# Split passes for the first S5 layer's products, with two u tiles and one tile of reordered states

## The chip, the cores and the metric

The kernel runs on one core of a Trainium2 chip. The metric is the device time of one execution, in microseconds (us). The core has TensorE (PE in the rows; PEld is its weight load), VectorE (DVE), ScalarE (ACT), GpSimd (POOL) and SyncE (SP), which mostly issues DMAs. Each engine runs its own instructions in the order in which they stand, and waits at one whose operands are not ready.

## The reference

The program is one inference step of a network of four layers over 128 context and 256 latent tokens, 384 together, of 1024 channels. Each layer norms its input, modulates it with a shift and a scale from a conditioning vector, mixes, gates and projects back. Layer 0 and layer 3 mix with an S5 state-space model, layer 1 pools, layer 2 attends. The S5 layer in its core:

```
u, z = split(h @ w_in, 2)                  # h: 384 x 1024, u and z: 384 x 2048
lam_bar = exp(lam * step)                  # for each of 128 groups, 64 states, 2 directions
b_bar = ((lam_bar - 1) / lam) * b
bu = einsum('blgc,gpc->blgp', u, b_bar)
states = associative_scan(a_r * a_l, a_r * b_l + b_r)   # forward and backward in time
y = d_skip * u + sum over directions of real(einsum(states, c))
y = gelu(y); y = y * sigmoid(y @ glu_w + glu_b)
out = (y * silu(z)) @ w_out
```

All arrays are float32.

## The kernel before

The first S5 layer is `S5Body.run`. Its 128 groups go in four blocks of 32. For block b, `u` (line 1074) multiplies h by four units of 128x1024 weights into three PSUM banks and VectorE transposes these into a tile of `Us`, one of three that blocks use in turn. `win` (four per block, q = 0 to 3) masks a quarter of the u tile on ScalarE (L1113), multiplies it by the input matrices on TensorE (L1122) and copies the result into E on ScalarE (L1125). E holds a block's states; two E buffers are used in turn, so block 2 needs the one of block 0. `rec` runs the scan in place in E: 63 steps of three VectorE operations (Pr, R, E; line 51 is the helper that issues them), where the first 32 steps work on two segments and the last 31, the half steps, on one.

When a block's scan is done, `out` makes four tiles of outputs (q = 0 to 3): `in_time` copies the states into an Eq tile in another order, with one copy of 64 partitions for each direction (L1185, L1188; on ScalarE, in block 3 the first of the two on VectorE), then TensorE multiplies in four groups Eq by P (L1212) and u by M (L1208), ScalarE applies the gelu (L1215) and issues the DMA of the result to yd. P and M are made on VectorE and TensorE by `S5Prep` from the layer's parameters. Eq has two buffers; in block 3 two tiles of `Us` stand in for two of its four Eq tiles.

z has sixteen units, each a product of 128x1024 weights with h on TensorE (L204), a silu on ScalarE (L1095) and a DMA; 3, 4, 3 and 6 of them are listed at the ends of the four scans.

The kernel has two ways to multiply in nearly float32. In `prod_a32` and `prod_b32` TensorE takes the float32 operands as they are, and each matmul leaves two records in the trace. In `prod_a` and `prod_b` each operand is the sum of a rounded high part and a low part, and three passes (high by high, high by low, low by high) are added in PSUM: `unit` casts the weights on ScalarE (whi, L138) and subtracts on VectorE (wlo, line 51). Before, the first S5 layer uses the former and all other layers the latter. The second S5 layer (`ahead`) has its own body, whose tables and some of whose low parts are made earlier and read back.

The ring of 128x1024 tiles has three slots each for whi and wlo. The tables of `S5Prep` in the first layer (W, and w1, w2, t) take slots of the same two names.

The order of the work on each engine is set by a list scheduler when the program is built: `run` gives it the steps of a block with the step of the scan at which each is listed, and it may move an instruction ahead of others on its engine where data allow.

Of the kernel before, what the change touches and what calls it, by code (L numbers as in the profile page):

```python
# [9 lines left out]
F32 = mybir.dt.float32  # L10
F32R = mybir.dt.float32r
# [19 lines left out]
class Net:  # L31
# [160 lines left out]
            if done:  # L192
                done(T, pss[T])

    def raw_unit(self, src):
        raw = self.ring.tile([128, 1024], F32, name="raw", tag="raw", bufs=4)
        self.nc.sync.dma_start(raw, src)
        return raw

    def prod_a32(self, ps, src, x):  # L200

        w = self.raw_unit(src)
        for k in range(8):
            self.nc.tensor.matmul(ps, w[:, k * 128:(k + 1) * 128], x[:, k, :], start=k == 0, stop=k == 7)  # L204

    def prod_b32(self, pss, wsrc, x):

        for u in range(4):
            w = self.raw_unit(wsrc[u])
            for k in range(2):  # L210
                kk = 2 * u + k
                for T, ps in enumerate(pss):
                    self.nc.tensor.matmul(ps, x[:, kk, T * 128:(T + 1) * 128], w[:, k * 512:(k + 1) * 512],  # L213
                                          start=kk == 0, stop=kk == 7)


    def rstd(self, xs, n, sqs):

# [41 lines left out]
    def modulated(self, l, hT, xn, natural=False):  # L260
# [3 lines left out]
        for k in range(8):  # L264
            ps = self.bank(self.sp, "sp")
            for T in range(3):
                nc.tensor.transpose(ps[:, T * 128:(T + 1) * 128], xn[:, T, k * 128:(k + 1) * 128], self.ident)
            p3 = ps[:, :NT].rearrange("p (t c) -> p t c", t=3)

            def put(out, act):  # L270
                o = out.rearrange("p (t c) -> p t c", t=3)
                if natural:

                    hv = o.rearrange("p t (c s) -> p t s c", s=4)
                    pv = p3.rearrange("p t (s c) -> p t s c", s=4)
                    dst, src = (hv[:, 0:2], hv[:, 2]), (pv[:, ::2], pv[:, 1])
                else:
                    dst, src = (o[:, ::2, :], o[:, 1, :]), (p3[:, ::2, :], p3[:, 1, :])
                for i in range(2):
                    sc, sh = m["sc"][:, k, i:i + 1], m["sh"][:, k, i:i + 1]  # L280
                    if act:
                        nc.scalar.activation(out=dst[i], in_=src[i], func=AF.Identity, scale=sc, bias=sh)
                    else:
                        nc.vector.tensor_scalar(out=dst[i], in0=src[i], scalar1=sc, scalar2=sh, op0=OP.mult, op1=OP.add)

            if hl is None:
                put(hh[:, k, :], k % 2)
                continue
            h = self.work.tile([128, 512], F32, name="h", tag="yo")[:, :NT]
            put(h, k % 2)  # L290
            if k % 2:
                nc.scalar.copy(out=hh[:, k, :], in_=h)
            else:
                put(hh[:, k, :], True)
            self.tt(hl[:, k, :], h, hh[:, k, :].bitcast(F32), OP.subtract)
# [161 lines left out]
    def s5(self, l, j, before, fill, ahead, side, between):  # L457
# [3 lines left out]
        with ExitStack() as outer:  # L461
# [7 lines left out]
            eps = [outer.enter_context(tc.tile_pool(name=f"ep{i}", bufs=1)) for i in range(2 if ahead else 1)]  # L469
            glu = Glu(self, j, yd, zd, eps)  # L470
            with ExitStack() as body:
                self.xn = eps[0].tile([128, 3, D], F32, name="xn", tag="e")
                h = []

                def start():
                    before()
                    xn = self.normed()
                    h.append(self.xp.tile([128, 8, NT], F32, name="h", tag="x"))
                    self.modulated(l, (h[0], None), xn)

                b = (S5Skewed if ahead else S5Body)(self, j, yd, zd, eps, body, ahead, start)
                if ahead:
                    before()
                    xn = self.normed()
                    h = [self.xp.tile([128, 8, NT], F32R, name="hh", tag="x"), b.sb.tile([128, 8, NT], F32R, name="hl")]
                    self.modulated(l, h, xn)
                b.run(h if ahead else h[0], fill, glu)
            self.x = self.xp.tile([128, 3, D], F32, name="x", tag="x")
            between()
            pp = outer.enter_context(tc.tile_pool(name="pp", bufs=1, side="right"))  # L490
# [541 lines left out]
class S5Body:  # L1032
# [3 lines left out]
    def __init__(self, net, j, yd, zd, eps, ctx, ahead, start):  # L1036
# [28 lines left out]
            self.prep.pair = lambda: (wq.tile([128, 4, 2, 64], F32, name="M", tag="M"),  # L1065
                                      wq.tile([128, 4, 64], F32, name="Md", tag="Md", bufs=1))
        self.eps = eps
        self.Us = [sb.tile([128, 16, 96], F32, name=f"U{i}") for i in range(3)]
        self.h0 = net.load(sb, A["h0"][j], [128, 64, 2, 2], "h0")
        nc.scalar.mul(out=self.h0[:, :, :, 1], in_=self.h0[:, :, :, 1], mul=-1.0)  # L1070
        self.fin = sb.tile([128, 64, 2, 2], F32, name="fin")
# [1 line left out]
    def u(self, b):  # L1073
# [1 line left out]
        n = self.n  # L1075
        pss = [n.bank(n.acc, "acc") for _ in range(3)]
        w = self.A["s5_wu"][self.j, b]
        if self.ahead:
            n.prod_b(pss, w, 4, *self.h, los=[self.ahead.lod[4 * b + u] if 4 * b + u < self.ahead.ulo else None for u in range(4)])
        else:  # L1080
            n.prod_b32(pss, w, self.h)
        U = self.Us[b % len(self.Us)]
        for T in range(3):
            self.nc.vector.transpose(out=U[:, :, T * 32:T * 32 + 32], in_=pss[T].rearrange("p (q c) -> p q c", c=32))
# [1 line left out]
    def z(self, q):  # L1086
        n, nc = self.n, self.nc
        ps = n.bank(n.acc, "acc")[:, :NT]
        w = self.A["s5_wz"][self.j, q]
        if self.ahead:  # L1090
            n.prod_a(ps, [w], 1, *self.h, los=[self.ahead.lod[16 + q] if q < self.ahead.zlo else None])
        else:
            n.prod_a32(ps, w, self.h)
        sz = n.work.tile([128, NT], F32, name="sz", tag="sz")
        nc.scalar.activation(out=sz.rearrange("p (s k c) -> p k s c", k=3, s=4),  # L1095
                             in_=ps.rearrange("p (k s c) -> p k s c", k=3, s=4), func=AF.Silu)
# [91 lines left out]
        nc.scalar.copy(out=ev[64:128, :, 3 - k - m:3 - k], in_=raw_ap(E[64:128], o, [[1, 16], [-33 * 64, m], [-64, 32]]))  # L1188

    def eq(self, b, qq):  # L1190
        if b == 3 and qq in (1, 2):
            return self.Us[qq]
        return self.wq.tile([128, 16, 96], F32, name="Eq", tag="Eq", bufs=1 if self.ahead else 2)

    def chunk_out(self, b, qq, P, M, Eq=None):

# [337 lines left out]
```

## Time and profile before

| what | value |
|---|---|
| median of three runs | 1810.89 us (1810.05 to 1817.27) |
| profiled execution | 1812.23 us, span 1810.4 us |
| mean granted clock of TensorE | 0.963 of full speed |
| busy: TensorE, VectorE, ScalarE | 1686.1, 1254.9, 978.3 us |

A row of a timeline gives the start from the span's beginning, the length, the engine, the line in the kernel, the operation, the tile written and those read with shapes, the number of instructions merged into it, and in brackets how long the engine idled before it and which engine's instruction ended that. The clock of TensorE is told as a share of 2.4 GHz. Ends of matmuls are modelled, so a last one shows its latency too. The first S5 layer's body runs from 47.6 to about 480 us: the first block's u and inputs to 80.8, scans of blocks 0 and 1 to 208.1, outputs of block 0 to 240.4, then inputs of block 2, and so on.

### The profile page before, as it was taken

Reading aid. Unit: us, or ns where it says so; the run is one execution under the profiler, and the core shown is the slowest. Engines: PE = TensorE matmul, PEld = TensorE weight load, DVE = VectorE, ACT = ScalarE, POOL = GpSimd, SP = SyncE. Lnnn points to the kernel's source line nnn. Section 1 sums busy time; section 2 is a strip of 40 time slices with the busy share of each in tenths; the row PEclk is TensorE's granted clock in tenths of the full one; section 3 lists DMA queues with packets and bytes.
Section 4 is the critical chain, followed back from the end, with each engine's and each line's share of the span. In section 5 each row is a group of like instructions: output and inputs, shape, how many; then the busy total and the mean of one; then the engine's idle time right before and its main releaser. Section 6 shows DMA issues by size and latency. Waiting matters only on the chain.

```text
span 1810.4 us, 29493 instructions
## 1 busy us (share of the span) xinstructions
PE 1686.1 (93%) x10928; PEld 1318.4 (73%) x10928; DVE 1254.9 (69%) x3149; ACT 978.3 (54%) x1588; POOL 5.4 (0%) x16
## 2 busy tenths in 40 slices
PE   4999999998999998999998999999899999899998
PEld 1464454654799977999887885657678778689986
DVE  7699876787476567888867737763439978656435
ACT  2653487636654455655546555642354777754322
POOL 0000000000000000000000000000000000000000
PEclk7999999997899998999998999999999999799999
DMA  8337767654577664655563566732567754567552
GB/s 311 98 119 240 228 182 220 195 180 137 166 252 231 193 205 135 188 162 163 179 218 113 186 205 229 239 127 82 181 226 226 227 182 140 166 232 213 172 165 72
DMA packets 174831, 334.30 MB, mean 185 GB/s; under 512 B 78528, under 2 KB 101856, under 8 KB 174688
## 3 DMA queue, kind: packets, MB, share of 16 engines
q1 hardware_dynamic: 165728, 319.84, 55.6%
q10 hardware_dynamic: 8960, 12.59, 2.1%
q8 instruction: 86, 1.41, 0.3%
q14 instruction: 57, 0.47, 0.1%
HBM read 279.54 MB, written 52.82 MB: 184 GB/s over the span
## 4 chain that ended last, share of the span: by engine, by line
PE 72%; DVE 9%; ACT 9%; DMA 6%; issue 3%; SPq 0%; ACTq 0%; DVEq 0%
PE acc L175 6%; PE acc L177 6%; PE acc L176 6%; PE sp L1122 4%; PE acc L829 4%; PE acc L830 4%; PE acc L831 4%; PE acc L213 3%; PE acc L159 3%; PE acc L160 3%; PE acc L161 3%; PE acc L204 3%; ACT Eq L1188 3%; DMA adw<-in_ada_w 2%; PE adps L99 2%
## 5 line engine op out<-in xcount | busy, mean ns | idle before, releaser
L51 DVE TENSOR_TENSOR wlo<-raw,whi 128x1024 fp32r<-128x1024 f32 (+2 forms) x234 | 281.2, 1204 | 246.3 <-ACT whi L138 229.0
L138 ACT CAST whi<-raw 128x1024 fp32r<-128x1024 f32 x246 | 257.6, 1050 | 315.2 <-PE acc L177 130.0
L51 DVE TENSOR_TENSOR Pr<-E,Tb 128x256 f32<-128x256 f32 (+1 forms) x504 | 173.9, 354 | 9.3 <-ACT E L1131 3.3
L159 PE MATMUL acc<-hh,whi 128*128 128x384 f32 x512 | 177.3, 347 | 0.2
L161 PE MATMUL acc<-hh,wlo 128*128 128x384 f32 x512 | 174.3, 340 | 0.3 <-DVE wlo L51 0.2
L160 PE MATMUL acc<-hl,whi 128*128 128x384 f32 x512 | 174.3, 340 | 0.0
L829 PE MATMUL acc<-y,whi 128*128 128x384 f32 x448 | 152.7, 345 | 8.1 <-ACT y L146 5.8
L831 PE MATMUL acc<-y,wlo 128*128 128x384 f32 x448 | 152.0, 340 | 1.0 <-DVE wlo L51 1.0
L830 PE MATMUL acc<-y,whi 128*128 128x384 f32 x448 | 152.7, 342 | 0.1
L175 PE MATMUL acc<-whi,ph 128*128 128x512 f32 x384 | 152.5, 397 | 0.0
L176 PE MATMUL acc<-wlo,ph 128*128 128x512 f32 x384 | 151.4, 394 | 0.0
L177 PE MATMUL acc<-whi,pl 128*128 128x512 f32 x384 | 151.3, 394 | 0.0
L51 DVE TENSOR_TENSOR E<-R,E 128x128 f32<-128x128 f32 (+1 forms) x504 | 123.1, 254 | 31.5 <-ACT E L1125 25.2
L51 DVE TENSOR_TENSOR R<-Pr 128x128 f32<-128x128 f32 (+1 forms) x504 | 123.7, 255 | 5.8
L159 PEld LDWEIGHTS acc<-hh,whi 128*128 128x128 f32 x512 | 97.1, 190 | 5.2 <-issue 2.0
L204 PE MATMUL acc<-h,raw 128*128 128x384 f32 x256 | 98.8, 516 | 0.0
L161 PEld LDWEIGHTS acc<-hh,wlo 128*128 128x128 f32 x512 | 96.8, 189 | 2.1 <-DVE wlo L51 0.9
L160 PEld LDWEIGHTS acc<-hl,whi 128*128 128x128 f32 x512 | 97.1, 190 | 1.0 <-issue 0.3
L99 PE MATMUL adps<-adw,scond 128*32 128x256 f32 x768 | 70.6, 422 | 27.7 <-DMA adw<-in_ada_w 27.3
L213 PE MATMUL acc<-raw,h 128*128 128x512 f32 x192 | 95.8, 617 | 0.0
L829 PEld LDWEIGHTS acc<-y,whi 128*128 128x128 f32 x448 | 84.6, 190 | 11.6 <-ACT y L146 7.1
L831 PEld LDWEIGHTS acc<-y,wlo 128*128 128x128 f32 x448 | 84.9, 190 | 2.2 <-DVE wlo L51 1.6
(285 smaller groups left out, 3261.6 us busy)
## 6 DMA issues: line engine op xcount, KB each, us to landing
adw<-in_ada_w SPq DMA_DIRECT2D x96, 512.0 KB
raw<-in_s_glu SPq DMA_DIRECT2D x64, 512.0 KB
raw<-in_s_wu SPq DMA_DIRECT2D x48, 512.0 KB
raw<-in_s_wz SPq DMA_DIRECT2D x40, 512.0 KB
raw<-in_s_wo SPq DMA_DIRECT2D x32, 512.0 KB
yq<-yd SPq DMA_DIRECT2D x64, 192.0 KB
lod<-wlo SPq DMA_DIRECT2D x24, 512.0 KB
wlo<-lod SPq DMA_DIRECT2D x24, 512.0 KB
```

The costliest lines, as they stand in the source:

```text
L51: return self.nc.vector.tensor_tensor(out=out, in0=a, in1=b, op=op)
L138: nc.scalar.copy(out=hi, in_=raw)
L159: nc.tensor.matmul(ps, h, xh[:, kk, :ncol], start=i == 0, stop=False)
L160: nc.tensor.matmul(ps, h, xl[:, kk, :ncol], start=False, stop=False)
L161: nc.tensor.matmul(ps, l, xh[:, kk, :ncol], start=False, stop=i == n - 1)
L175: nc.tensor.matmul(ps, xh[:, kk, xs], h, start=kk == 0, stop=False)
L176: nc.tensor.matmul(ps, xh[:, kk, xs], l, start=False, stop=False)
L177: nc.tensor.matmul(ps, xl[:, kk, xs], h, start=False, stop=kk == 2 * nu - 1)
L204: self.nc.tensor.matmul(ps, w[:, k * 128:(k + 1) * 128], x[:, k, :], start=k == 0, stop=k == 7)
L829: self.nc.tensor.matmul(ps, h, y[:, 0, k], start=u == 0 and k == 0, stop=False)
L830: self.nc.tensor.matmul(ps, h, y[:, 1, k], start=False, stop=False)
L831: self.nc.tensor.matmul(ps, l, y[:, 0, k], start=False, stop=u == 1 and k == 7)
```

## The change

The first S5 layer takes the same way as the others: `u` calls `prod_b` and `z` calls `prod_a`, with no low parts prepared (`los` is a list of None). `modulated` therefore makes h in two parts, hh and hl; the plain branch and the two float32 products are removed, and `start` is the same for both layers. hl takes a tile of 12 KB in each partition. `Us` has two tiles in place of three in the first layer, so that block 2 takes the tile of block 0 and block 3 that of block 1, and Eq one buffer in place of two. In block 3 only q = 1 has a u tile as its Eq.

```diff
@@ class Net
-    def raw_unit(self, src):
-        raw = self.ring.tile([128, 1024], F32, name="raw", tag="raw", bufs=4)
...
-    def prod_a32(self, ps, src, x):
...
-    def prod_b32(self, pss, wsrc, x):
...
@@ def modulated
-            if hl is None:
-                put(hh[:, k, :], k % 2)
-                continue
             h = self.work.tile([128, 512], F32, name="h", tag="yo")[:, :NT]
@@ the S5 layer
+                hlp = body.enter_context(tc.tile_pool(name="hlp", bufs=1))
...
-                    h.append(self.xp.tile([128, 8, NT], F32, name="h", tag="x"))
-                    self.modulated(l, (h[0], None), xn)
+                    h.extend([self.xp.tile([128, 8, NT], F32R, name="hh", tag="x"), hlp.tile([128, 8, NT], F32R, name="hl")])
+                    self.modulated(l, h, xn)
...
@@ class S5Body
-        self.Us = [sb.tile([128, 16, 96], F32, name=f"U{i}") for i in range(3)]
+        self.Us = [sb.tile([128, 16, 96], F32, name=f"U{i}") for i in range(3 if ahead else 2)]
...
-        if self.ahead:
-            n.prod_b(pss, w, 4, *self.h, los=[self.ahead.lod[4 * b + u] if 4 * b + u < self.ahead.ulo else None for u in range(4)])
-        else:
-            n.prod_b32(pss, w, self.h)
+        lo = lambda i: self.ahead.lod[i] if self.ahead and i < self.ahead.ulo else None
+        n.prod_b(pss, w, 4, *self.h, los=[lo(4 * b + u) for u in range(4)])
...
-        if self.ahead:
-            n.prod_a(ps, [w], 1, *self.h, los=[self.ahead.lod[16 + q] if q < self.ahead.zlo else None])
-        else:
-            n.prod_a32(ps, w, self.h)
+        n.prod_a(ps, [w], 1, *self.h, los=[self.ahead.lod[16 + q] if self.ahead and q < self.ahead.zlo else None])
...
-        if b == 3 and qq in (1, 2):
-            return self.Us[qq]
-        return self.wq.tile([128, 16, 96], F32, name="Eq", tag="Eq", bufs=1 if self.ahead else 2)
+        if b == 3 and qq in ((1, 2) if self.ahead else (1,)):
+            return self.Us[qq if self.ahead else 0]
+        return self.wq.tile([128, 16, 96], F32, name="Eq", tag="Eq", bufs=1)
```

The removed lines shift those behind them: L1185, L1188, L1208, L1212 and L1084 of before are L1154, L1157, L1177, L1181 and L1056 after. The scheduler then gives another order on each engine. Three places follow, with the rows before first and those after second; the number behind a name counts tiles, so one tile has different numbers in the two.

On ScalarE, at the end of the first block's scan (E_615 before, E_646 after), where the outputs of block 0 begin; M is the matrix for u, yc the gelu's result:

```order
L1153 ACTIVATE fin_614<-E_616 128x32 x2
L1185 COPY Eq_1963<-E_615 64x1536
L1188 COPY Eq_1963<-E_615 64x1536
L1185 COPY Eq_1999<-E_615 64x1536
L1188 COPY Eq_1999<-E_615 64x1536
L957 ACTIVATE M_1991<-Md_1992,masks_91 128x4x64
L1215 ACT_TABLE_LOAD
L1215 ACTIVATE yc_1987<-tp_1966 128x384
L957 ACTIVATE M_1991<-Md_1992,masks_91 128x4x64
L1219 DMA yd0_120<-yc_1987 4x16x384 x2
L1215 ACTIVATE yc_2023<-ad_2002 128x384
L1185 COPY Eq_2035<-E_615 64x1536
```

```order
L1154 COPY Eq_2182<-E_646 64x1536
L1157 COPY Eq_2182<-E_646 64x1536
L1122 ACTIVATE fin_645<-E_647 128x32 x2
L931 ACTIVATE M_2210<-Md_2211,masks_91 128x4x64
L1184 ACT_TABLE_LOAD
L1184 ACTIVATE yc_2206<-tp_2185 128x384
L931 ACTIVATE M_2210<-Md_2211,masks_91 128x4x64
L1188 DMA yd0_120<-yc_2206 4x16x384 x2
L1154 COPY Eq_2218<-E_646 64x1536
L1157 COPY Eq_2218<-E_646 64x1536
```

Before, four copies into two Eq tiles stand in a row, and the third tile's stand behind two gelus. After, two copies stand ahead of the first gelu, and each next tile's two copies stand behind the one before it.

On TensorE, ahead of the first products of block 1's outputs (Eq_3077 before, Eq_3440 after); adps is the product of the next layer's conditioning, sp that of `win`:

```order
L1122 MATMUL sp_2934<-U1_2912,W_2897 64x96 x4
L1122 MATMUL sp_2944<-U0_2910,W_2897 64x96 x4
L1122 MATMUL sp_2944<-U1_2912,W_2897 64x96
L99 MATMUL adps_2719<-adw_2740,scond_85 32x256 x4
L1122 MATMUL sp_2944<-U1_2912,W_2897 64x96 x3
L1212 MATMUL tp_3080<-Eq_3077,P_2163 64x96 x4
L1208 MATMUL tp_3080<-U1_609,M_2188 128x96
L1212 MATMUL tp_3080<-Eq_3077,P_2163 64x96 x4
```

```order
L160 MATMUL acc_3399<-hl_433,whi_3402 128x384
L161 MATMUL acc_3399<-hh_432,wlo_3403 128x384
L159 MATMUL acc_3399<-hh_432,whi_3402 128x384
L160 MATMUL acc_3399<-hl_433,whi_3402 128x384
L161 MATMUL acc_3399<-hh_432,wlo_3403 128x384
L1181 MATMUL tp_3443<-Eq_3440,P_2446 64x96 x4
L1177 MATMUL tp_3443<-U1_641,M_2471 128x96
L1181 MATMUL tp_3443<-Eq_3440,P_2446 64x96 x4
L1177 MATMUL tp_3443<-U1_641,M_2471 128x96
```

Before, the inputs of block 2 (win, L1122) stand right ahead of these products. After, it is the last of four z products (acc_3399), three of whose like stand above it.

On VectorE, near the end of block 3's scan (E_616 before, E_647 after), the last P, the output matrix:

```order
L51 TENSOR_TENSOR Pr_4920<-E_616,Tb_132 128x128
L51 TENSOR_TENSOR R_4921<-Pr_4920 128x2x32
L51 TENSOR_TENSOR E_616<-R_4921,E_616 128x64
L1185 COPY Eq_4927<-E_616 64x1536
L1185 COPY U1_609<-E_616 64x1536
L51 TENSOR_TENSOR adarow_4587<-adps_4586,adarow_4587 128x256
L51 TENSOR_TENSOR P_4659<-C_4657,Lf_133 128x512 x2
L51 TENSOR_TENSOR t_4660<-C_4657,Lf_133 128x512 x2
L51 TENSOR_TENSOR P_4659<-P_4659,t_4660 128x512 x2
```

```order
L51 TENSOR_TENSOR E_647<-R_5030,E_647 128x64
L51 TENSOR_TENSOR Pr_5034<-E_647,Tb_135 128x128
L51 TENSOR_TENSOR P_5146<-C_5144,Lf_136 128x512
L51 TENSOR_TENSOR R_5035<-Pr_5034 128x2x32
L51 TENSOR_TENSOR P_5146<-C_5144,Lf_136 128x512
L51 TENSOR_TENSOR E_647<-R_5035,E_647 128x64
L51 TENSOR_TENSOR P_5146<-P_5146,t_5147 128x512
L51 TENSOR_TENSOR Pr_5039<-E_647,Tb_135 128x128
L51 TENSOR_TENSOR P_5146<-P_5146,t_5147 128x512
L51 TENSOR_TENSOR R_5040<-Pr_5039 128x2x32
```

Before, the last step of the scan, the two copies and a sum stand ahead of the last P. After, that P (P_5146) stands between steps of the scan, 24 half steps ahead of its end.

## Rows read from the trace of the kernel before

**Rows 1.** The page: busy time, share of the span and instructions; then the chain's shares.

```profile
PE 1686.1 (93%) x10928; PEld 1318.4 (73%) x10928; DVE 1254.9 (69%) x3149; ACT 978.3 (54%) x1588; POOL 5.4 (0%) x16
...
PE 72%; DVE 9%; ACT 9%; DMA 6%; issue 3%; SPq 0%; ACTq 0%; DVEq 0%
```

**Rows 2.** First layer by stretch: stretch, length, busy of each engine, PE clock, DMA.

```profile
47.60:80.80 33.20, 30.67 (x95) 13.91 (x96) 19.28 (x43) 22.24 (x71) 1.68 (x2) 0.93 0.21 63
80.80:208.10 127.30, 122.71 (x1029) 65.97 (x1029) 114.07 (x382) 51.48 (x110) 0.15 (x1) 1.00 0.62 196
208.10:240.40 32.30, 28.94 (x228) 17.36 (x226) 21.59 (x57) 29.63 (x19) 0.15 (x1) 1.00 0.58 174
240.40:304.20 63.80, 60.28 (x621) 34.05 (x621) 45.23 (x128) 56.05 (x78) 0.00 (x0) 1.00 0.66 198
304.20:392.50 88.30, 86.31 (x732) 48.42 (x731) 76.39 (x277) 34.56 (x72) 0.15 (x1) 1.00 0.70 223
392.50:452.40 59.90, 47.96 (x309) 28.44 (x308) 41.55 (x143) 43.05 (x45) 0.00 (x0) 0.74 0.38 114
sum 404.80, PE 376.88 PEld 208.16 DVE 318.11 ACT 237.02 POOL 2.14; mean PE 62.81 PEld 34.69 DVE 53.02 ACT 39.50 POOL 0.36
```

**Rows 3.** Timeline, TensorE, the products now: start, length, engine, line, operation, records, [idle].

```profile
104.08 14.86 PE L213 MATMUL acc<-raw,h 128*128 128x512 f32 x34
...
206.40 2.85 PE L204 MATMUL acc<-h,raw 128*128 128x384 f32 x8
```

**Rows 4.** Timeline, TensorE, split passes of later layers.

```profile
718.92 0.33 PE L159 MATMUL acc<-hh,whi 128*128 128x384 f32 x1
...
720.48 0.34 PE L159 MATMUL acc<-hh,whi 128*128 128x384 f32 x1
...
1320.76 0.40 PE L175 MATMUL acc<-whi,hh 128*128 128x512 f32 x1
...
1322.15 0.39 PE L175 MATMUL acc<-whi,hh 128*128 128x512 f32 x1
```

**Rows 5.** Groups by shape, first 500 us: count | busy us, mean ns | idle.

```profile
L51 DVE TENSOR_TENSOR wlo<-raw,whi 128x1024 fp32r<-128x1024 f32 x7 | 8.4, 1222 | 15.5 <-ACT whi L138 9.0 <-DMA szq<-zd 6.5
L138 ACT CAST whi<-raw 128x1024 fp32r<-128x1024 f32 x8 | 8.3, 1043 | 7.3 <-DMA szq<-zd 3.7 <-PE acc L830 2.8 <-PE sp L830 0.8
```

**Rows 6.** Timeline, ScalarE, first block's outputs.

```profile
208.14 2.90 ACT L1185 COPY Eq<-E 64x1536 f32<-64x1536 f32 x1 [2.96 <-DVE E L51]
211.05 2.92 ACT L1188 COPY Eq<-E 64x1536 f32<-64x1536 f32 x1
213.99 2.90 ACT L1185 COPY Eq<-E 64x1536 f32<-64x1536 f32 x1
...
220.34 1.28 ACT L1215 ACT_TABLE_LOAD   x1
...
240.44 0.24 ACT L1131 COPY E<-h 128x64 f32<-128x64 f32 x1
```

**Rows 7.** Timeline, TensorE, one output tile at either clock.

```profile
230.07 0.55 PE L1212 MATMUL tp<-Eq,P 128*64 128x96 f32 x8 [1.48 <-ACT Eq L1188]
...
232.69 0.55 PE L1212 MATMUL tp<-Eq,P 128*64 128x96 f32 x8
...
415.78 0.91 PE L1212 MATMUL tp<-Eq,P 128*64 128x96 f32 x8 [4.52 <-ACT Eq L1188]
...
420.32 0.91 PE L1212 MATMUL tp<-Eq,P 128*64 128x96 f32 x8
```

**Rows 8.** Timeline, VectorE, third and fourth blocks.

```profile
283.84 0.29 DVE L51 TENSOR_TENSOR E<-R,E 128x128 f32<-128x128 f32 x1 [7.24 <-ACT E L1125]
...
316.21 0.72 DVE L1084 STREAM_TRANSPOSE U<-acc 128x512 f32<-128x512 f32 x1 [0.41 <-PE acc L213]
...
447.90 0.29 DVE L51 TENSOR_TENSOR Pr<-E,Tb 128x128 f32<-128x128 f32 x1
...
452.72 0.23 DVE L51 TENSOR_TENSOR E<-R,E 128x64 f32<-128x64 f32 x1
```

More of the change, by code (lines that the diff above doesn't have):

```diff
@@ L193, in prod_b @@
                 done(T, pss[T])
-    def raw_unit(self, src):
-        raw = self.ring.tile([128, 1024], F32, name="raw", tag="raw", bufs=4)
-        self.nc.sync.dma_start(raw, src)
-        return raw
-    def prod_a32(self, ps, src, x):
-        w = self.raw_unit(src)
-        for k in range(8):
-            self.nc.tensor.matmul(ps, w[:, k * 128:(k + 1) * 128], x[:, k, :], start=k == 0, stop=k == 7)
-    def prod_b32(self, pss, wsrc, x):
[L208 to L214, printed above, removed]
     def rstd(self, xs, n, sqs):
@@ L477, in start @@
                     xn = self.normed()
-                    h.append(self.xp.tile([128, 8, NT], F32, name="h", tag="x"))
-                    self.modulated(l, (h[0], None), xn)
+                    h.extend([self.xp.tile([128, 8, NT], F32R, name="hh", tag="x"), hlp.tile([128, 8, NT], F32R, name="hl")])
+                    self.modulated(l, h, xn)
                 b = (S5Skewed if ahead else S5Body)(self, j, yd, zd, eps, body, ahead, start)
                 if ahead:
[L483 to L487, printed above, removed]
+                    start()
+                b.run(h, fill, glu)
             self.x = self.xp.tile([128, 3, D], F32, name="x", tag="x")
```

## The prediction

> **What bounds the kernel now.** I read the page's first part and its chain first. TensorE is busy 93% of the span and holds 72% of the chain, VectorE 69% and 9% [rows 1]. That average covers four layers, and the change touches only the first, which lies between 47.6 and about 480 us. So the second view is the table by stretch [rows 2]. In the stretches where scans run (80.8 to 208.1 and 304.2 to 392.5 us) TensorE is busy 122.7 of 127.3 and 86.3 of 88.3 us, but VectorE is nearly as full: 114.1 of 127.3 and 76.4 of 88.3. Over the six stretches VectorE is idle 404.8 - 318.1 = 86.7 us. A busy TensorE here is partly work put into gaps: the scan is a chain of steps of three VectorE operations that nothing shortens. At its end, six half steps run from 447.90 to 452.95, 0.84 us each, with nothing between them [rows 8].
>
> The third view is the timeline of each engine where a block of the scan hands over. After the first block's last step, ScalarE reorders the states in a row of copies: 208.14, 211.05, 213.99, each 2.9 us, started by VectorE's E [rows 6]. The next scan in the same E buffer gets its first column at 240.44 [rows 6] and its last block of inputs at 283.84, after 7.24 us in which VectorE waited for ScalarE's copy [rows 8]. So the layer is set by a relay: scan (VectorE), copies (ScalarE), small products (TensorE), inputs of the scan after next (all three), scan again.
>
> **The change part by part.**
>
> *The products on TensorE.* u: 96 float32 matmuls, 192 records. 34 records take 14.86 us, the last one ending late by its own length, so (14.86 - 0.62)/33 = 0.43 us a record and 83 us in all; z: 8 records in 2.85, so 0.33, and 256 x 0.33 = 85 us [rows 3]. Split in three, u has 288 passes at (1322.15 - 1320.76)/6 = 0.232, 67 us, and z 384 at (720.48 - 718.92)/9 = 0.173, 67 us [rows 4]. TensorE has 34 us less to do. I count them as no gain in themselves, because the relay and not the queue of products sets the end; they can be worth between 0 and -34.
>
> *The splits.* Each of the 32 units of weights now needs one cast on ScalarE (1.04 us) and one subtraction on VectorE (1.22 us) before its matmuls [rows 5]: 33 us of ScalarE and 39 us of VectorE. The modulated input gets its own low part: 8 subtractions of 128x384, which the trace shows here in no such form; a third of the length of the 128x1024 one is 0.4 us, a half 0.6, so 3 to 5 us of VectorE, and about 4 of ScalarE. VectorE carries some 42 us more. The bounds of what of that lengthens the layer are 0 (all inside the 86.7 us idle) and 42.
>
> *One tile of reordered states for two.* In the first order piece ScalarE now fills one Eq, and can't fill the next before TensorE has read the first. Each tile costs 5.8 us of copies [rows 6] and then 4 groups of products, from 230.07 to about 233.5, 3.5 us at full clock; where the clock was half, from 415.78 to about 422, 6 us [rows 7]. Before, the copies of the next tile hid the groups.
>
> *Two u tiles for three.* Block 2's u now lands in block 0's tile, so its three transposes (0.72 us each [rows 8]) wait until the last product of out(0) has read it; block 3's wait for out(1). In out(3) one u tile in place of two takes reordered states. The low parts and the scan's own tables share a ring of three slots, so a table can wait for a product's last pass; I allow 0 to 7 us for that and take none.
>
> A rule speaks the other way. TensorE's weight loads are busy 73%, VectorE 69% [rows 1]. The Trainium skill, Perfetto Trace Analysis, Identifying the Most-Contended Engine, says to find the engine with the highest occupancy, TensorE judged by its weight loads, and to relieve that first. On the whole page this picks TensorE, and the sum would be -34. By stretch, weight loads are 208 of 405 us and VectorE 318 [rows 2]; the same rule read there picks VectorE, which the change loads. I go by the stretches.
>
> The relay after the change, on the profiled run's clock:
>
> 1. Scan 0 ends at 208.1 now. Ahead of it stand 11 of the 32 subtractions, 13 us, and about 5 us of the new input work: 226. Stretch 2 has 13 us of idle VectorE, so this could be as little as +5.
> 2. out(0): four times 5.8 us of copies, between them three times 3.5 us of groups and about 1 us of signals and M, and the table load 1.3 [rows 6]: 38 us, to 264. The last group (3.5) and the three transposes (2.1) bring block 2's input work to 270. It started at 240.4.
> 3. The inputs of block 2 took 240.4 to 283.8, 43 us, with 11 of copies and activations of out(0) and z mixed in; these are gone from there, so 32: 302. Already +18.
> 4. out(1) stands on TensorE behind four z products now (second order piece; TensorE runs in order): 96 x 0.173 = 17 us, which begin when their subtractions are made. First group done at 323, three more tiles at 5.8 + 3.5 + 1 and a table, 355, transposes 357. They stood at 316.2 + 0.7 [rows 8]: +40. Queued behind these transposes on VectorE is scan 2 itself, with 34 of its 63 steps to go.
> 5. Inputs of block 3, 36 us: 393. The rest of scan 2 runs beside them and ends by about 416, where it ended at 392.5: +23.
> 6. out(2): 38 + 3.5 = 457 at full clock, 467 at half; I take 460.
> 7. In the third order piece the output matrix of out(2)'s last products' slot, P, is rewritten in the middle of scan 3, and 24 half steps stand behind it on VectorE. P waits for that product; then 24 x 0.84 = 20, six subtractions 7 and a few sums of the next product's input, 4: 491. Scan 3 ended at 452.95: +38.
> 8. out(3) has one tile less to copy into: between 0 and +4. ScalarE is by then also behind later work, and I leave the total at +38.
>
> As a cross-check, VectorE's own sum is +42 with its idle time unchanged; the two counts share no term but the subtractions. Everything after the layer is the same work, so it moves as a whole. The profiled execution took 1812.23 us for a span of 1810.4, and the median of the runs is 1810.89, 1.3 less. So 1812.2 + 38 - 1.3 = 1849; I give 1848.
>
> **Rivals.**
>
> *TensorE is the bound after all.* For it: 93% busy and 72% of the chain [rows 1], 86.3 of 88.3 in stretch 5. Mechanism: products fill TensorE up to each hand-over, splits go into the 86.7 us of VectorE's idle time, and the relay moves up with them. It decides if the subtractions fit into VectorE's waits, that is, if z's go out before the scan ends rather than at it. Price: -34, so 1777, and 1780 to 1790 if out's copies give back part. Against it: stretch 6, where TensorE is 12 us idle, and the order pieces.
>
> *The splits hide, the products aren't the bound.* VectorE idle 86.7 against 42; the single Eq tile's groups (four blocks of three groups, 3.5 each, 42 us) would be paid for by the 34 us saved. Sum about +2 to +8: 1812 to 1819. Against it: the idle of VectorE is scattered, and its longest part comes after the scans, where the relay already waits.
>
> *The clock falls.* In stretch 6 the granted clock was 0.74, with TensorE busy 48 of 60 us; in the four others before it 1.00 [rows 2]. With 34 us less work in a layer 38 us longer, TensorE has more pauses in every stretch. At 1.2 instead of 2.4 GHz the z products ahead of out(1) cost 17 more and each of four outputs 2.5 more on its exposed last group, 10 in all: +27 on top, 1875. For it: the row of 415.78. Against it: TensorE keeps over 85% of its work.
>
> *The change doesn't do what it says.* The scheduler still puts three blocks' u into the air: excluded by the code, two tiles are two tiles.
>
> **How the numbers follow.** Likeliest, chance 0.62: the relay with splits in it, 1848, its own range 1828 to 1866 (step 1 at +5 gives 13 less, table waits 7 and half clock in out(2) 10 more). Clock falls as well: 0.20, 1860 to 1880. Splits hide: 0.10, 1810 to 1822. TensorE the bound: 0.08, 1777 to 1800. A measurement of this kernel can't tell less than 0.5%, 9 us, from no change: faster is under 1802, slower over 1820. Faster 0.08, same 0.09, slower 0.83. The range leaves out the TensorE case, half of the hidden case and the top of the clock case: 1815 to 1876.
>
> **What would show it.** In the changed profile the subtractions number 32 more at about 1.2 us, and TensorE is busy some 34 us less. The first copy of out(0) starts near 226. Copies of Eq stand apart in pairs with TensorE's L1181 as the releaser of the second pair. The transposes L1056 of block 3 come near 357. Scan 3 ends near 491, and from there to the end both traces run in parallel. The prediction is wrong if scan 0 ends before 212, if the layer's scans end less than 15 us later, or if the difference arises after the layer, in code that the change doesn't touch.

## The result: 74 us slower, and the profile after

The changed kernel takes 1884.87 us (median of four, 1884.52 to 1886.11) against 1810.47 for the kernel before: 1.0414 times as long, interval 1.0396 to 1.0433. The forecast was 1848, +38, with a range of 1815 to 1876. The sign was right; the size was half, and the time lies above the range.

The first part of the page of the changed kernel, busy time and then the chain's shares:

```profile
PE 1682.5 (89%) x11152; PEld 1376.9 (73%) x11152; DVE 1300.2 (69%) x3189; ACT 1014.7 (54%) x1632; POOL 5.4 (0%) x16
...
PE 66%; ACT 11%; DVE 11%; DMA 8%; issue 3%; ACTq 0%; SPq 0%; DVEq 0%
```

Against [rows 1] VectorE has 45.3 us more work (1300.2 - 1254.9), and its idle time, span less busy, rose from 555.5 to 583.1, by 27.6. TensorE's busy time hardly moved (1682.5 for 1686.1), although by the prediction's estimate it has 34 us less to do at full clock: from 47.6 us to scan 3's end its mean granted clock fell from 0.96 to 0.83, and that took the saving back. The table by stretch says where, cut at the same events as [rows 2]: prelude, first two scans, outputs of block 0, inputs of block 2, scan 2 with out(1), then out(2) and scan 3.

```profile
47.60:80.80 33.20, 28.94 (x121) 19.20 (x121) 21.64 (x48) 25.57 (x75) 1.69 (x2) 0.87 0.23 78
80.80:231.10 150.30, 117.90 (x1123) 81.88 (x1122) 128.63 (x387) 64.69 (x131) 0.15 (x1) 0.92 0.60 183
231.10:277.10 46.00, 21.82 (x152) 15.62 (x152) 31.44 (x88) 33.29 (x28) 0.15 (x1) 0.54 0.15 40
277.10:316.70 39.60, 36.33 (x450) 25.55 (x450) 21.84 (x64) 31.84 (x59) 0.00 (x0) 0.86 0.49 147
316.70:448.40 131.70, 113.09 (x999) 79.80 (x998) 105.61 (x320) 70.17 (x102) 0.15 (x1) 0.91 0.63 202
448.40:531.10 82.70, 60.49 (x425) 46.38 (x426) 61.71 (x180) 50.90 (x58) 0.00 (x0) 0.69 0.42 121
sum 483.50, PE 378.58 PEld 268.42 DVE 370.88 ACT 276.46 POOL 2.14; mean PE 63.10 PEld 44.74 DVE 61.81 ACT 46.08 POOL 0.36
```

The first scans take 150.3 us for 127.3, with VectorE 14.6 us busier and TensorE idle for 32 us where it was idle for 4.6. During the outputs of block 0 TensorE works 21.8 of 46.0 us at a granted clock of 0.54, where it had 1.00 [rows 2]. VectorE's idle time in the layer up to scan 3's end goes from 86.8 to 112.6 us.

ScalarE's timeline at the first output tiles of block 0:

```profile
231.08 2.84 ACT L1154 COPY Eq<-E 64x1536 f32<-64x1536 f32 x1 [36.48 <-DVE E L51]
233.92 2.82 ACT L1157 COPY Eq<-E 64x1536 f32<-64x1536 f32 x1
...
243.26 0.49 ACT L1184 ACTIVATE yc<-tp 128x384 f32<-128x384 f32 x1
...
245.50 2.82 ACT L1154 COPY Eq<-E 64x1536 f32<-64x1536 f32 x1 [1.35 <-issue]
```

It answers to [rows 6]: the second tile's copies begin 14.4 us after the first's, not 5.8. TensorE's timeline of the same tiles:

```profile
236.80 0.91 PE L1181 MATMUL tp<-Eq,P 128*64 128x96 f32 x8 [17.55 <-ACT Eq L1157]
...
241.33 0.91 PE L1181 MATMUL tp<-Eq,P 128*64 128x96 f32 x8
...
251.20 0.91 PE L1181 MATMUL ad<-Eq,P 128*64 128x96 f32 x8 [6.25 <-ACT Eq L1157]
```

The four groups run from 236.8 to 242.2, 5.4 us, the length that [rows 7] show at half clock. VectorE's timeline at the transposes of block 2, around the start of scan 2, at the transposes of block 3, and at the last step of scan 3:

```profile
280.37 1.91 DVE L1056 STREAM_TRANSPOSE U<-acc 128x512 f32<-128x512 f32 x3 [2.25 <-PE ad L1177]
...
309.66 2.36 DVE L51 TENSOR_TENSOR wlo<-raw,whi 128x1024 fp32r<-128x1024 f32 x2 [0.67 <-ACT whi L138]
316.77 0.29 DVE L51 TENSOR_TENSOR E<-R,E 128x128 f32<-128x128 f32 x1 [4.75 <-ACT E L1094]
317.10 0.42 DVE L51 TENSOR_TENSOR Pr<-E,Tb 128x256 f32<-128x256 f32 x1
317.56 0.29 DVE L51 TENSOR_TENSOR R<-Pr 128x128 f32<-128x128 f32 x1
317.76 1.22 DVE L51 TENSOR_TENSOR wlo<-raw,whi 128x1024 fp32r<-128x1024 f32 x1
318.90 0.28 DVE L51 TENSOR_TENSOR E<-R,E 128x128 f32<-128x128 f32 x1
...
385.68 1.91 DVE L1056 STREAM_TRANSPOSE U<-acc 128x512 f32<-128x512 f32 x3 [1.40 <-PE ad L1177]
...
531.18 0.23 DVE L51 TENSOR_TENSOR E<-R,E 128x64 f32<-128x64 f32 x1
```

The scan's R at 317.56 and its E at 318.90 have a subtraction between them, so that they start 1.34 us apart; in steps without one it is 0.32 to 0.33. The products of z that stand ahead of out(1), and what goes with them, run in this stretch:

```profile
316.70:340.20 23.50, 22.13 (x157) 16.34 (x156) 20.46 (x54) 6.80 (x10) 0.00 (x0) 1.00 0.89 293
```

TensorE's clock is 1.00 there. Scan 3 ends at 531.4, where [rows 8] had 452.95. Three of VectorE's waits from 47.6 to 531.1 (total us, times, longest) show the new idle time:

```profile
DVE Tt L917 <- ACT Tt L915: 20.7, 12, 5.8
DVE w L51 <- PE acc L176: 15.7, 7, 6.1
DVE wlo L51 <- ACT whi L138: 14.7, 14, 5.3
```

The first was 3.4 us before; the other two are new. From the last output products of the layer (562.4 for 490.5) to the end both kernels run alike, 1321 and 1320 us.

### The profile page after: what moved, and what is told of

Read it like the earlier page. It is cut to its first block, busy times and chain, and to the rows that moved or that the text cites. A ratio compares the mean times of both kernels' runs of the same rounds, so it can differ in the third digit from the quotient of the medians.

```text
span 1883.3 us, 30096 instructions
## 1 busy us (share of the span) xinstructions
PE 1682.5 (89%) x11152; PEld 1376.9 (73%) x11152; DVE 1300.2 (69%) x3189; ACT 1014.7 (54%) x1632; POOL 5.4 (0%) x16
## 4 chain that ended last, share of the span: by engine, by line
PE 66%; ACT 11%; DVE 11%; DMA 8%; issue 3%; ACTq 0%; SPq 0%; DVEq 0%
PE acc L175 7%; PE acc L176 7%; PE acc L177 7%; PE acc L159 4%; PE acc L160 4%; PE sp L1091 4%; DMA adw<-in_ada_w 4%; PE acc L161 4%; PE acc L804 3%; PE acc L803 3%; PE acc L805 3%; ACT Eq L1157 3%; DVE wlo L51 2%; PE adps L99 2%; PE tp L1181 2%
## 5 line engine op out<-in xcount | busy, mean ns | idle before, releaser
L51 DVE TENSOR_TENSOR wlo<-raw,whi 128x1024 fp32r<-128x1024 f32 x266 | 320.1, 1206 | 255.8 <-ACT whi L138 243.0
L138 ACT CAST whi<-raw 128x1024 fp32r<-128x1024 f32 x278 | 290.8, 1050 | 366.6 <-PE acc L177 136.9
L159 PE MATMUL acc<-hh,whi 128*128 128x384 f32 x640 | 222.2, 347 | 0.3 <-ACT whi L138 0.2
L161 PE MATMUL acc<-hh,wlo 128*128 128x384 f32 x640 | 219.7, 344 | 2.4 <-DVE wlo L51 2.4
L160 PE MATMUL acc<-hl,whi 128*128 128x384 f32 x640 | 220.4, 344 | 0.0
L176 PE MATMUL acc<-wlo,ph 128*128 128x512 f32 x384 | 151.4, 394 | 0.0
L161 PEld LDWEIGHTS acc<-hh,wlo 128*128 128x128 f32 x640 | 121.5, 190 | 10.7 <-issue 5.2
L51 DVE TENSOR_TENSOR R<-Pr 128x64 f32<-128x64 f32 (+1 forms) x504 | 121.3, 254 | 6.3
L1154 ACT COPY Eq<-E 64x1536 f32<-64x1536 f32 x24 | 70.4, 2935 | 55.6 <-DVE E L51 48.7
L175 PE MATMUL acc<-whi,hh 128*128 128x512 f32 (+1 forms) x216 | 89.2, 414 | 1.9 <-ACT hh L261 1.9
L176 PE MATMUL acc<-wlo,hh 128*128 128x512 f32 (+1 forms) x216 | 89.3, 414 | 0.0
```

What stands on the lines that cost most here:

```text
L51: return self.nc.vector.tensor_tensor(out=out, in0=a, in1=b, op=op)
L138: nc.scalar.copy(out=hi, in_=raw)
L159: nc.tensor.matmul(ps, h, xh[:, kk, :ncol], start=i == 0, stop=False)
L160: nc.tensor.matmul(ps, h, xl[:, kk, :ncol], start=False, stop=False)
L161: nc.tensor.matmul(ps, l, xh[:, kk, :ncol], start=False, stop=i == n - 1)
L175: nc.tensor.matmul(ps, xh[:, kk, xs], h, start=kk == 0, stop=False)
```

## The experiments

Each was timed against the kernel before; "over before" is the difference of medians within one comparison, behind it the ratio's interval in per cent. The edits are shown shortened to what acts in the first S5 layer, which is meant by "first layer".

**What the buffers cost: e1, e2, e3.** e1 is the kernel before with both `Us` and `eq` of the change, e2 with the second of the two lines alone, e3 with two u tiles (and one of them as Eq in block 3) and Eq left at two buffers:

```diff
-for i in range(3)]
+for i in range(3 if ahead else 2)]
-tag="Eq", bufs=1 if self.ahead else 2)
+tag="Eq", bufs=1)
```

Expected of e1: 

> The kernel before with float32 products, but two u tiles and one Eq tile. If the single tiles of the relay cost the time (one Eq at a time, TensorE waiting and slow meanwhile): 40 to 60 us over before, with outputs of blocks 0 to 2 some 14 us a tile apart. If the splits on VectorE cost it: within 0 to 15 us of before.

Expected of e2: 

> The kernel before with one Eq tile, three u tiles kept. Buffers: 30 to 50 us over before, since it is Eq that puts copies and products in a row. Splits: 0 to 10 us.

Expected of e3: 

> The kernel before with two u tiles, two Eq tiles kept. Buffers: 3 to 20 us over before, the transposes of blocks 2 and 3 wait for the outputs, and their inputs after them; less than the Eq tile alone. Splits: 0 to 5 us.

Measured: e1 +14.2 us (0.6 to 1.2%), e2 +13.5 (0.6 to 1.1%), e3 +6.9 (0.2 to 0.6%). The tiles of e1's first outputs do stand 14.5 us apart, as in the change (copies at 205.2 and 219.7), yet the sum is a quarter to a third of the 40 to 60 that the theory of the single tiles expected. That they make the loss by themselves is out; e6 below shows that they can cost more beside the passes. e1 to scan 3's end, and from there to the last output products:

```profile
47.60:485.60 438.00, 396.51 (x3133) 226.53 (x3133) 341.30 (x1044) 245.83 (x406) 2.14 (x5) 0.94 0.58 177
485.60:509.40 23.80, 21.84 (x206) 17.98 (x204) 8.69 (x8) 19.25 (x15) 1.59 (x1) 1.00 0.50 168
```

Scan 3 does end 33 us later than before (485.9), but the last output products follow after 23.8 us and not 37.6, so that much of the delay is taken back.

**The splits with the buffers of before: e4.** The changed kernel with three u tiles and two Eq; h's low part is subtracted in place, and the middle pass takes the high part again, so that one term is left out:

```diff
-h.extend([self.xp.tile([128, 8, NT], F32R, name="hh", tag="x"), hlp.tile([128, 8, NT], F32R, name="hl")])
+h.extend([hh, hh])
-self.tt(hl[:, k, :], h, hh[:, k, :].bitcast(F32), OP.subtract)
+self.tt(h, h, hh[:, k, :].bitcast(F32), OP.subtract)
```

Expected: 

> The split passes with the three u tiles and two Eq tiles of before; room is made by leaving out h's low part (its subtractions are made, but the middle pass multiplies by the high part again, so that one term is missing from the result). Buffers: 10 to 25 us over before. Splits: 55 to 75 us over before, like the change itself. If TensorE were the bound: 20 to 35 us under before.

Measured: +70.1 us (3.5 to 4.4%), not apart from the change (4.0 to 4.3%). So the single tiles add some 4 us, if anything, to a kernel that has the splits. Its stretch from 47.6 us to the end of scan 3:

```profile
47.60:509.90 462.30, 358.69 (x3171) 249.91 (x3172) 366.15 (x1079) 270.15 (x438) 2.14 (x5) 0.85 0.51 156
```

VectorE is busy 366.2 for 318.5 and idle 96.2 for 86.8: the loss up to there is 57 us, 48 of them VectorE's work.

**Which part of the splits: e5, e6, e7.** In e5 `unit` makes no low part for the first layer and the high part stands for it, in e6 it makes neither part, and in e7 the float32 way of before makes both and uses none:

```diff
e5, unit:
+if nolo: lo = hi
e6, unit:
+if nolo: return self.stand, self.stand     # part of hh
e7, raw_unit:
+self.nc.scalar.copy(out=hi, in_=raw)
+self.tt(lo, raw, hi.bitcast(F32), OP.subtract)
```

Expected of e5: 

> The changed kernel without the 32 subtractions of weights on VectorE (the high part stands for the low one, so that term is missing from the result); casts, three passes, hl and single tiles stay. If VectorE's work costs the time: 40 to 55 us under the changed kernel, 1830 to 1845. If it is the wait of the products for cast and low part in a row: 15 to 35 under it, since the cast still stands there. If it is the single tiles: under 10.

Expected of e6: 

> The changed kernel without casts and subtractions: the weights are loaded and not used, part of hh stands for both parts of them (the products are of wrong numbers). Three passes, hl and single tiles stay. All theories of the splits: 55 to 90 us under the changed kernel, 1795 to 1830, the passes then being 34 us less on TensorE than in the kernel with single tiles and float32 products (1827). If the saving on TensorE is worth nothing in itself: 1820 to 1830; if it is worth all: 1793.

Expected of e7: 

> The kernel before with the 32 casts and 32 subtractions made and not used by anything: float32 products, three u tiles, two Eq. If VectorE's and ScalarE's time is what the splits cost: 40 to 60 us over before. If it is that products wait for cast and subtraction in a row: 5 to 20 us over before.

Measured over before: e5 +40.0 us (1.7 to 2.6%), e6 +52.2 (2.6 to 3.4%), where the change has +74.4; e7 +59.8 (3.1 to 3.7%). e7 is the clearest: nothing reads its casts and subtractions, TensorE does the products of before, and four fifths of the loss are there. Taking pieces out of the change gives less. Without subtractions (e5) it is 34 us faster (74.4 less 40.0), short of the 40 to 55 expected of VectorE's work alone. VectorE's wait at the subtraction for the cast, up to scan 3's end of e7:

```profile
DVE wlo L51 <- ACT whi L199: 16.9, 8, 8.3
```

A subtraction whose cast isn't done holds up all that stands behind it on VectorE, scan steps among it. e6 fits no theory: every one expected 55 to 90 us under the change, and it is 22 under; it has less work than e5 and takes 12 longer. It is the kernel before with single tiles (e1, +14.2), passes (e13 below, +11.9) and h's low part (e16, +3.0), which add up to 29, and it costs 52. Its stretch to scan 3's end, in an execution of 1856.2 us where the median is 1866.0:

```profile
47.60:506.90 459.30, 394.54 (x3401) 283.93 (x3402) 347.32 (x1055) 254.29 (x421) 2.15 (x5) 0.88 0.56 173
```

VectorE is idle 112.0 us there, as long as in the change (112.6), without one split in it. So the splits suffice for 60 us, but the single tiles with the passes and h's low part cost 52 without them; the two overlap in the change, and what each has of the 74 is not shown.

**Is it the half clock: e8.** Twenty passes of u by M ahead of each output tile, overwritten later:

```diff
+for _ in range(20 if i == 0 and not self.ahead else 0):
+    nc.tensor.matmul(yp[:, c], M[:, i].rearrange("p g t -> p (g t)"), U[:, 4 * qq + i, :], start=True, stop=True)
```

Expected: 

> The changed kernel with 20 more passes of u by M ahead of each output tile's products, overwritten by the right ones, so that TensorE has work while the reordered states are copied. If the half clock in the output stages costs 10 to 27 us: the groups take 3.5 us again and the time falls by 5 to 20. If the clock follows the pauses and costs nothing: within 5 us, or up to 10 over from the added passes.

Measured: 1895.9 us, +82.1 over before (4.3 to 5.0%), so in no case faster than the change. Of the TensorE timeline in out(0), the added passes and the first and last group of the next tile:

```profile
241.88 6.86 PE L1178 MATMUL tp<-U,M 128*128 128x96 f32 x40 [1.96 <-ACT M L931]
...
249.02 0.55 PE L1183 MATMUL ad<-Eq,P 128*64 128x96 f32 x8
...
251.63 0.55 PE L1183 MATMUL ad<-Eq,P 128*64 128x96 f32 x8
```

The groups now take 3.2 us (249.02 to 252.18), and out(2) ends 11.5 us earlier than in the change (486.5 for 498.0). Scan 3 ends 6.7 later (538.1 for 531.4). The gain of the clock was there and was lost again. The run is no clean test: to scan 3's end TensorE is busy 431.7 us, 53 more than in the change, with the added passes; whether they or the other order lost the gain, it doesn't tell. That the clock makes the loss is not shown, nor what part of it.

**Shared slots: e9, and GpSimd: e10.** e9 gives w1, w2 and t three slots of their own, with h's low part as in e4. e10 subtracts the first layer's weights on GpSimd:

```diff
e9:
-return net.ring.tile([128, 1024], F32, name=k, tag="whi" if k == "W" else "wlo")
+return sb.tile([128, 1024], F32, name=k, tag="tab", bufs=3)     # W stays in the ring
e10, unit:
+(nc.gpsimd if nolo else nc.vector).tensor_tensor(out=lo, in0=raw, in1=hi.bitcast(F32), op=OP.subtract)
```

Expected of e9: 

> The changed kernel, but the tables w1, w2 and t have three slots of their own in place of those of the low parts; room for them comes from h's low part, which is subtracted in place and not used (the middle pass takes the high part again, so that term is missing). In the changed kernel VectorE waited 15.7 us in the first layer for passes that read a low part, ahead of writing w. If this wait, from shared slots, is on the path: 10 to 25 us under the changed kernel. If only VectorE's work counts: within 5 of it.

Expected of e10: 

> The changed kernel with the 32 subtractions of the first layer's weights on GpSimd instead of VectorE; all else as in the change. If VectorE's time and its waits at the subtraction (14.7 us for casts) cost the time: 25 to 45 us under the changed kernel, about 1840 to 1860. If GpSimd's subtractions are slow or slow VectorE down: 0 to 20 under, or above.

Measured over before: e9 +69.5 us (3.5 to 4.3%), which is not apart from the change; e10 +87.2 (4.5 to 5.0%), which is slower than it. e9 missed the 10 to 25 under the change, e10 the 25 to 45. In e9's waits of VectorE the wait of w for the pass L176 is gone, and others have grown:

```profile
DVE P L51 <- PE tp L1184: 16.9, 5, 4.9
...
DVE U L1059 <- PE acc L177: 12.1, 3, 8.8
```

In the change P waited 13.1 us for those products, and the transposes into U had no such wait. The waiting moved and the sum stayed. For e10, first two groups of scan steps in the change, to 560 us, then GpSimd's subtraction and the same steps in e10:

```profile
L51 DVE TENSOR_TENSOR Pr<-E,Tb 128x256 f32<-128x256 f32 x128 | 53.5, 419 | 2.4 <-ACT E L1100 0.9
...
L51 DVE TENSOR_TENSOR R<-Pr 128x128 f32<-128x128 f32 x128 | 36.4, 286 | 1.4
```

```profile
L140 POOL TENSOR_TENSOR wlo<-raw,whi 128x1024 fp32r<-128x1024 f32 x32 | 77.5, 2432 | 310.0 <-ACT whi L138 182.2 <-DVE Pr L51 55.6 <-DVE R L51 39.6
L51 DVE TENSOR_TENSOR Pr<-E,Tb 128x256 f32<-128x256 f32 x128 | 70.6, 554 | 2.5 <-ACT E L1100 0.3
...
L51 DVE TENSOR_TENSOR R<-Pr 128x128 f32<-128x128 f32 x128 | 49.7, 391 | 1.9
```

32 subtractions take 2.43 us each on GpSimd, and the scan's steps lengthen, in the mean from 419 to 554 ns and from 286 to 391. The mean hides how: nine Pr take 2.4 to 2.6 us, about as long as a subtraction, and the 113 that meet none take 0.42 as in the change. One of either, with the subtraction that it met:

```profile
113.97 2.50 POOL L140 TENSOR_TENSOR wlo<-raw,whi 128x1024 fp32r<-128x1024 f32 x1 [0.70 <-ACT whi L138]
...
114.24 2.51 DVE L51 TENSOR_TENSOR Pr<-E,Tb 128x256 f32<-128x256 f32 x1
...
117.44 0.43 DVE L51 TENSOR_TENSOR Pr<-E,Tb 128x256 f32<-128x256 f32 x1
```

**One product alone: e11, e12.** As e4, with u, or z, again a float32 product:

```diff
e11:
+n.prod_b32(pss, w, self.h[0].bitcast(F32))
e12:
+n.prod_a32(ps, w, self.h[0].bitcast(F32))
```

Expected of e11: 

> Split passes for z alone, u as a float32 product of h's high part, three u tiles and two Eq as before, h's low part left out. If the loss is VectorE's work: half of the loss of both splits with these buffers (70), 30 to 40 over before. If it is u, which stands on the path from scan to scan: under 20.

Expected of e12: 

> Split passes for u alone, z as a float32 product of h's high part, three u tiles and two Eq as before, h's low part left out. VectorE's work: 30 to 40 over before. u on the path from scan to scan: over 50. z ahead of the outputs: under 20.

Measured: z alone +39.8 us (1.8 to 2.4%), u alone +42.4 (2.1 to 2.6%), both (e4) +70.1. Sixteen units cost alike, those of u and those of z, and sixteen more add about 29, 1.8 us each. That u costs more because it stands between the scans (over 50 expected) is out.

**Each piece by itself in the kernel before: e13 to e16.** e13 has three passes on part of hh, with no cast, no subtraction and no low part of h, and the buffers of before; e14 only the cast of e7; e15 only a subtraction that waits for nothing; e16 only the work of h's low part, with its casts:

```diff
e14, raw_unit:
+self.nc.scalar.copy(out=hi, in_=raw)
e15, raw_unit:
+self.tt(lo, raw, raw, OP.subtract)
e16, modulated:
+self.tt(h, h, hh[:, k, :], OP.subtract)
```

Expected of e13: 

> Three passes in place of float32 matmuls with three u tiles and two Eq, with no cast, no subtraction and no low part of h: weights are loaded and not used, part of the one rounded h stands for them (wrong numbers). If TensorE were the bound: 25 to 35 us under before. If the relay sets the end: within 10 of before. If the passes bring about the remainder by themselves (other order, slower clock): 15 to 30 over.

Expected of e14: 

> The kernel before with the 32 casts alone made on ScalarE and not used. If only VectorE's work counts: within 5 us of before. If ScalarE's queue is on the path, too: 15 to 30 over.

Expected of e15: 

> The kernel before with 32 subtractions alone on VectorE (of the raw weights from themselves), not used and waiting for no cast. If VectorE's work counts one for one: 32 x 1.22 = 39, 33 to 45 over before. If the 60 of casts and subtractions together were all VectorE's queue: 50 to 60. If they fit into its idle time: under 15.

Expected of e16: 

> The kernel before with h's 8 low parts made in place and not used (with the casts that go with them); h itself stays float32. It stands ahead of the first u, where nothing hides it: 5 to 12 us over before. If hidden: under 3.

Measured over before: e13 +11.9 us (0.5 to 0.9%), e14 +5.4 (0.2 to 0.7%), e15 +43.1 (2.2 to 2.8%), e16 +3.0 (0.1 to 0.4%). The stretch of e13 up to scan 3's end:

```profile
47.60:456.50 408.90, 355.33 (x3192) 252.35 (x3193) 317.10 (x1023) 235.81 (x391) 2.14 (x5) 0.89 0.55 173
```

TensorE is busy 22 us less than before (377.4) at a clock of 0.89 for 0.96, and the stretch is 3.6 us longer: shorter products alone bring nothing. The casts alone cost 5 us, not the 15 to 30 of a ScalarE on the path; with e15 that makes 48.5, and e7, in which each subtraction also waits for its cast, has 11 more. e15's VectorE in the middle of scan 0, then its stretches to scan 3's end and to the last output products:

```profile
143.91 1.22 DVE L51 TENSOR_TENSOR wlo<-raw 128x1024 fp32r<-128x1024 f32 x1
145.04 0.28 DVE L51 TENSOR_TENSOR E<-R,E 128x128 f32<-128x128 f32 x1
145.25 1.22 DVE L51 TENSOR_TENSOR wlo<-raw 128x1024 fp32r<-128x1024 f32 x1
146.38 0.42 DVE L51 TENSOR_TENSOR Pr<-E,Tb 128x256 f32<-128x256 f32 x1
...
47.60:483.20 435.60, 382.02 (x2992) 210.37 (x2992) 346.29 (x1055) 235.08 (x394) 2.14 (x5) 0.90 0.52 161
483.20:532.00 48.80, 42.40 (x279) 31.93 (x280) 30.43 (x37) 28.70 (x32) 1.59 (x1) 0.84 0.61 200
```

Each of the two lies between operations of the scan and delays the next by 1.13 us (145.25 to 146.38). 18 of the 32 stand inside a scan like this, six behind scan 3's end. Scan 3 ends 30 us later than before, with 26 of them (32 us) ahead of it, and the last output products come 41.5 later (532.0 for 490.5). All 32 last 39 us, and 43 came out: they count in full. The clock is 0.90 for 0.96 in the first stretch; its part isn't told apart.

**Less of both: e17, e18.** The sums P<-P,t are left out of the first layer, in the kernel before and in e13:

```diff
+if j:
     n.tt(p1[:, 0], p1[:, 0], p2[:, 1], OP.add)
     n.tt(p1[:, 1], p1[:, 1], p2[:, 0], OP.subtract)
```

Expected of e17: 

> The kernel before without the 32 sums of P and t in the first layer's output matrices (the matrices are wrong; 32 x 0.685 = 22 us of VectorE). If VectorE's work counts one for one in both directions: 16 to 25 us under before. If VectorE and TensorE are both at their limit in turn: 3 to 12 under. If VectorE has slack in before and only became the bound by the splits: within 3.

Expected of e18: 

> The same sums left out of the kernel with passes alone (no casts, subtractions or low part of h; part of the rounded h stands for the weights). VectorE one for one: 16 to 25 under the kernel with passes alone, near 1800. Both engines in turn: 30 to 45 under it, since the 34 us of TensorE then come into effect. Slack: no change.

Measured: e17 -3.0 us against before (-0.4 to 0.0%), e18 +8.5 (0.3 to 0.8%), 3 us under e13. The stretch of e17 up to scan 3's end:

```profile
47.60:457.30 409.70, 381.67 (x3023) 212.39 (x3022) 307.63 (x994) 236.79 (x394) 2.13 (x5) 0.95 0.58 177
```

VectorE is busy 307.6 us, 11 less than before (the sums had overlapped their neighbours in part), and idle 102.1, 15 more; this execution took 1817.2 us, the longest of ten, with a median of 1809.5. Subtractions added to VectorE count in full (e15); these sums, taken away, came back as idle time. So the layer isn't bound by VectorE's sum in both directions.

## Why the prediction had the sign and not the size

The step that failed is the price of the splits in the relay. It counted 17 of the 32 subtractions, 20 us, put the other 15 at nothing, and had no term for a subtraction that waits for its cast. The runs show 43 us for the 32 subtractions (e15) and 60 with the casts in front of them (e7).

*TensorE's saving is worth nothing in itself:* right. e13 takes it alone and is 11.9 slower; the rival of -34 is out, and so is the one in which the splits hide (e15); e18 shows that the saving doesn't come into effect with less VectorE work either.

*The splits lengthen the layer through VectorE:* right in mechanism, too small in size. The relay priced 11 subtractions in step 1 and six in step 7. In the changed trace 15 stand ahead of scan 0's end, four of them for the first u, and six in step 7; two stand just ahead of scan 2 (309.7 and 310.8 us), and nine inside it (six to 355, three between 413 and 422), in steps for which I had priced none.

*The cross-check, "+42 with its idle time unchanged", failed.* The work was right (45.3), the idle time grew by 27.6. That it agreed with the relay was no support, since both left out the waiting. I had set the wait for shared slots at 0 to 7 and taken none; it was 15.7, but e9, which removes it, is not apart from the change, so that wait is not shown to be the error. The wait for the cast was not among my terms at all (14.7 in the change, 16.9 in e7). Nor is it the whole: e6 has no cast and as much idle time.

*The single tiles:* their mechanism is in the trace, at half clock even longer than I said. But I made them the frame of the relay and took the delay at scan 3's end for that of the whole. In e1 that delay is 33 us, and 14.2 are left of it; on top of the splits the single tiles cost 4.3, and beside passes without splits some 37 (e6 less e13 and e16). My steps against the trace, in us from the span's start:

| step | before | forecast | measured |
|---|---|---|---|
| 1, scan 0 ends | 208.1 | 226 | 231.1 |
| 2, transposes of block 2 | 200.4 | 270 | 282.3 |
| 3, inputs of block 2 | 283.8 | 302 | 316.7 |
| 4, transposes of block 3 | 316.9 | 357 | 387.6 |
| 5, scan 2 ends | 392.5 | 416 | 448.4 |
| 6, out(2) done | 428.6 | 460 | 498.0 |
| 7, scan 3 ends | 453.0 | 491 | 531.4 |
| last output products | 490.5 | | 562.4 |

Of the 40 us between forecast and trace at scan 3's end 16 arise in step 4, 7 in step 2, 6 in step 6 and 5 in step 1. Step 2 took 51.2 us for 44: four groups of 5.4 instead of 3.5, the half clock. Step 4 took 71 for 55, with six of those subtractions in it. The clock's rival was right in one of its two terms: the groups of out(0) and out(2) ran slowly (0.54 and 0.69 in the two stretches with them), but the z products ahead of out(1), which it priced at 17 us more, had a clock of 1.00. The groups explain parts of the relay, but e8 puts them back to 3.2 us and is not faster.

Two sums of the prediction are off without changing this: by [rows 7] a tile's groups at half clock end at 421.2, 5.4 us and not 6, and 13 us less than 1848 is 1835, not the 1828 given as the lower end.

*The sum of the parts.* Alone they give 59.8 (casts and subtractions) + 11.9 (passes) + 3.0 (h) = 74.7 where e4 has 70.1; with the buffers' 14.2 it is 88.9 where the change has 74.4. The splits' parts add up within the noise; the buffers' cost is mostly covered in the change. That the parts add up is no rule here: by the same sum e6 would be 29, and it is 52.

Open stay four things: why passes alone cost 12; why e6, with less to do than e5, takes 12 us longer, and 23 more than its parts (in both, the scheduler's order differs as well, and no run held it fixed); what part of the loss is the clock's; and which waits set the kernel before, where neither less VectorE work, nor less TensorE work, nor both gain over 3 us.

## What to carry to other kernels

An engine's idle time is no room for added work when that work joins the in-order queue of a serial chain: here 32 operations of 1.22 us, 18 of them between the steps of a scan, cost 43 us, though the engine had 87 us idle in the layer, and 60 when each also had to wait for another engine first. Price such an edit first as count times length, then add the wait in front; take a discount only for those that demonstrably stand in an existing wait. A cheap test comes before the change: issue the new work without using it. And test the parts together as well as alone: here the sum of the parts held for one set of them and missed by 23 us for another.

## What the runs showed of the hardware

A float32 product of 128x512 took two records of 0.43 us each [rows 3], the three split passes 0.23 each [rows 4]: 0.86 against 0.70, so the gain on TensorE was small from the start.

GpSimd was slower (2.43 us for 1.22) and no spare engine. With its subtractions in the layer VectorE's busy time in the whole run is 1328.1 us, 28 more than in the change, with 32 subtractions fewer. The Trainium skill, GPSIMD Engine Reference, Specifications, says that its memory interfaces are shared with VectorE and contended by VectorE instructions with two inputs from on-chip memory; the scan's steps agree: Pr reads E and Tb, and one that met a subtraction took 2.51 us for 0.43.

In the changed kernel TensorE's granted clock went to 0.54 in a stretch where it worked 21.8 of 46.0 us, and its busy time over the layer (378.6 us to scan 3's end, 377.4 before) hid that its work had shrunk, by an estimated 34 us.
